# Down products whose operands begin elsewhere: split weights at 192, activations at 0 modulo 256 bytes

## The chip, the cores and the metric

The kernel runs on one core of one Trainium2 chip, from one program. The metric is the device time of one execution in microseconds (us). The kernel before takes 406.14 us, the median of three runs (405.77 to 406.33).

## The reference

One layer of a decoder for a sequence of S = 256 positions and a width of D = 1024, all in float32:

```
h = rmsnorm(x); proj = h @ w_in
x = x + (sigmoid(gA) * (o_A @ w_proj_nsa) + sigmoid(gB) * (o_B @ w_proj_dil)) @ w_out
h = rmsnorm(x)
u, gate = split(h @ w_up)            # w_up: 1024 x 5632
uc = conv_b + causal depthwise conv of width 3 over u
x = x + (gelu(uc) * gate) @ w_down   # w_down: 2816 x 1024
return rmsnorm(x)
```

o_A is a sparse attention (compressed, selected and sliding-window branches, gated), o_B a dilated attention over three groups. The change touches the last product but one line, `@ w_down`, alone.

## The kernel before

**Products in three parts.** Every float32 operand of a large product is split into a high part (`hi`, `ah`, `hTh`: the value rounded to the format fp32r) and a low part (the rest: `lo`, `al`, `hTl`). A product is then high x high + high x low + low x high, three matmuls that add up in PSUM. Names in the profile: `whi` and `wlo` are the split weights, `raw` the weights as they come from memory.

**Units.** The work is a list of units in the order of the program, each with one block of weights of 128 x 2048 numbers (1 MB). A unit's weights are loaded by a DMA of SP's queue into one of three `raw` buffers, split by ACT (`split_hi`, L128) and DVE (`split_lo`, L132) into one of three `whi` and three `wlo` buffers, and used by PE. Loads are issued five units ahead, the split runs one to two units ahead. `Unit` has a parameter `o`: the number of elements by which the unit's split weights begin behind the start of their buffers (buffers have 2240 elements, 2048 are used). Before, it is 32 in the three units of the values of the dilated attention (`vb`), and 0 elsewhere.

**Feed-forward part.** For each of NF = 11 blocks j of 256 hidden channels there are three units: two up products (for u and for gate) and one down product. The down product of block j - 2 stands behind the up products of block j, and the last two down products are computed at the end, by quarters of the output (function `last`).

- An up product is 2 x 8 x 3 = 48 matmuls (L177 and L182 in `parts`). The moving operand is hTh or hTl, 128 rows x 256 positions, and the stationary operand a piece of 128 x 128 of `whi` or `wlo`. They write `ps_d` for even j and `ps_o` for odd j.
- A down product is 48 matmuls too (L630 in `mm_down_part`). The moving operand is a row piece of 256 of `whi` or `wlo`, and the stationary one a piece of 128 x 128 of the activations `ah` or `al`. The same piece is loaded four times in succession, for four pieces of weights that go to four regions of PSUM, in `ps_s` or in the two `ps_t`.
- Between them the other engines work on the block: U = the scaled up product with two columns of zeros ahead (L581), C = the convolution (L585 on ACT, L589 on DVE) and its gelu (L596, L597), M = C times the gate (L604), and `ah`, `al` = its split (L614, L615).

A unit of `kick` in `parts` is one extra matmul of 64 columns ahead of a product, at two places of the program. It stays as it is.

**Where the tiles lie.** A matmul's operands are at a byte address in each partition of SBUF. By the built program, modulo 256:

| operands | before | after |
|---|---|---|
| up products: moving hTh, hTl | 192 | 192 |
| up products: stationary whi, wlo | 0 | 0 |
| down products: moving whi, wlo | 0 | 192 |
| down products: stationary ah, al | 64 | 0 |
| products of `vb` (o=32): moving whi, wlo; stationary hTh, hTl | 128; 192 | 128; 192 |
| third product (L177, ps_s): moving whi, wlo; stationary hTh, hTl | 0; 192 | 0; 192 |
| products for the merge and the output: moving oah, ob, mixh; stationary whi, wlo | 192; 0 | 192; 0 |
| C, M | 64 | 0 |
| U, its two buffers | 0, 32 | 0, 0 |

Each piece of an operand begins a multiple of 256 bytes behind the tile's start, so that a tile's number holds for all its pieces.

Of the kernel before, what the change touches and what calls it, by code (L numbers as in the profile page):

```python
# [11 lines left out]
F32 = mybir.dt.float32  # L12
# [6 lines left out]
S = 256  # L19
D = 1024  # L20
DFF = 2816
NF = DFF // 256
# [71 lines left out]
def build(ctx, tc, a, out):  # L94
# [9 lines left out]
    def pd(shape, tag="d"):  # L104
        return ps.tile([128] + shape, F32, name="ps_" + tag, tag=tag, bufs=1 if tag == "s" else 2)
# [91 lines left out]
    def CW(w, t):  # L197
        return sm_[:, 38 + 22 * w + t:39 + 22 * w + t]
# [29 lines left out]
    def bc(R, n):  # L228
        return R[:, None, :].to_broadcast([128, n, R.shape[-1]])
# [346 lines left out]
    def ev_u(j):  # L576
        def f(u):
            f_ = ffn["pool"]
            U = f_.tile([128, 2, S + 2], F32, name="U", tag="U", bufs=2)
            V.memset(U[:, :, 0:2], 0.0)  # L580
            V.tensor_tensor(out=U[:, :, 2:], in0=u.p, in1=bc(rt["R2"], 2), op=OP.mult)  # L581
            C = f_.tile([128, 2, S], F32, name="C", tag="C", bufs=2)
            for c in range(2):
                t = 2 * j + c
                A.activation(C[:, c], U[:, c, 2:], AF.Identity, scale=CW(2, t), bias=CB[:, t:t + 1])  # L585
            for w in (1, 0):
                for c in range(2):
                    t = 2 * j + c
                    V.scalar_tensor_tensor(C[:, c], U[:, c, w:w + S], CW(w, t), C[:, c], op0=OP.mult, op1=OP.add)  # L589
            ffn["C", j] = C  # L590
        return f
# [27 lines left out]
    def mm_down_part(u, j, tcs, c0=0, c1=512, own=None):  # L619

        wh, wl = w3(u, 2)
        h, l = ffn["a", j]
        half = [(0, 256), (256, 512)] if c1 - c0 == 512 else [(c0, c1)]
        start, seen = j == (0 if own is None else NF - 2), set()
        for n, (w, x) in enumerate(((wh, h), (wh, l), (wl, h))):
            for t in sorted({t for t, _ in tcs}):
                for kt in range(2):
                    for ch in [ch for q, ch in tcs if q == t]:
                        for b, e in half:
                            T.matmul(ffn["y"][t][ch][:, b:e] if own is None else own, x[:, kt, t * 128:t * 128 + 128],  # L630
                                     w[:, kt, ch * 512 + b:ch * 512 + e], start=start and (t, ch) not in seen,
                                     stop=j == NF - 1 and n == 2 and kt == 1, skip_group_check=True)
                            seen.add((t, ch))

    def mm_down(j):
        def f(u):
            if j == 0:
                s2 = pd([2, 512], "s")
                ta = pd([512], "t")
                tb = pd([512], "t")  # L640
                ffn["y"] = [[s2[:, 0], s2[:, 1]], [ta, tb]]
            if j < NF - 2:
                mm_down_part(u, j, [(t, ch) for t in range(2) for ch in range(2)])
        return f
# [12 lines left out]
        return f  # L657

    NFIRST = len(units)
    downs = [Unit(2048, mm_down(j)) for j in range(NF)]  # L660
    for j in range(NF + LAG):
        if j < NF:
            units.append(Unit(2048, mm_up(j, 0), ev_u(j)))
# [586 lines left out]
```

## Time and profile before

| | us |
|---|---|
| median of three runs | 406.14 |
| the profiled execution: its span from the first to the last instruction | 404.7 |
| PE busy / PE weight loads busy | 394.7 / 383.2 |
| DVE busy | 291.2 |
| ACT busy | 212.4 |
| POOL busy | 31.2 |
| first down product's first row in the chain of waits | at 248.32 |
| end of the last down matmul | at 397.7 |

The profiled execution's time beyond its span was not recorded, so the 1.4 us between its span and the median of the runs stand for what lies around the span.

How to read the rows: PE is the engine of the matmuls, PEld its loading of the stationary operand, which runs beside the matmuls. DVE, ACT and POOL are the vector, scalar and general engines, and SP issues DMAs. A row of the chain of waits has start, length, engine, tile, line and a count. Matmuls overlap in the pipeline, so the duration of one (277 ns, for instance) is not the time that it costs. What it costs is the time from one start to the next, and that is the length of a row of the chain divided by its count. A row of the grouped view has line, engine, operation, tiles, shapes and count, then busy us and mean ns of one, then the idle time ahead.

### The profile page before, as it was taken

The page shows a single profiled execution, that of the slowest core. Times are in us where ns is not written, and L with a number is a line of the kernel's source. Part 1 is how long each engine was busy: PE and PEld are TensorE (multiplying, and loading weights), DVE is VectorE, ACT ScalarE, POOL GpSimd, SP SyncE. Part 2 cuts the span into 40 slices and gives each one's busy share as a digit, 9 for nine tenths or more (in the row PEclk, how much of TensorE's full clock was granted, in tenths as well). Part 3 has the DMA queues.
Part 4 walks back from the last instruction along what each step waited for, and adds up shares of the span by engine and source line. Part 5 has one row for each costly group of instructions (what it writes and reads, how often), then busy time and mean ns, then how long its engine had stood idle before and what let it go on. Part 6 is the DMA issues. An engine that isn't in the chain of part 4 may idle for free.

```text
span 404.7 us, 8015 instructions
## 1 busy us (share of the span) xinstructions
PE 394.7 (98%) x3412; PEld 383.2 (95%) x3412; DVE 291.2 (72%) x486; ACT 212.4 (52%) x293; POOL 31.2 (8%) x58
## 2 busy tenths in 40 slices
PE   8999989999999999999999999999999999999993
PEld 6999989999998989999999999999999999999992
DVE  5879889887786557458897499676594774946853
ACT  5776764366664345663554765445264352643512
POOL 7100000000000000061143000000000000000012
PEclk9999999999999999999999999999999999999997
DMA  8965746345332532343556346662734726438002
GB/s 319 390 251 207 249 168 209 105 158 220 144 105 105 201 113 105 131 181 108 206 208 235 130 136 236 255 222 108 296 119 194 266 99 261 160 152 299 15 0 105
DMA packets 10980, 72.59 MB, mean 179 GB/s; under 512 B 1216, under 2 KB 1472, under 8 KB 2880
## 3 DMA queue, kind: packets, MB, share of 16 engines
q1 hardware_dynamic: 10512, 70.96, 48.2%
q10 hardware_dynamic: 432, 1.11, 0.7%
q8 instruction: 27, 0.44, 0.4%
q14 instruction: 9, 0.07, 0.1%
HBM read 71.02 MB, written 1.05 MB: 178 GB/s over the span
## 4 chain that ended last, share of the span: by engine, by line
PE 83%; DVE 10%; ACT 2%; DMA 2%; issue 1%; SPq 0%; POOLq 0%; POOL 0%; ACTq 0%
PE ps_d L177 25%; PE ps_d L182 12%; PE ps_o L177 9%; PE ps_s L630 8%; PE ps_t L630 7%; PE ps_o L182 5%; DVE wlo L132 4%; DMA first<-in_first_dram 2%; PE ps_t L177 2%; DVE hTl L202 2%; PE ps_d L344 2%; PE ps_o L905 2%; PE ps_s L946 1%; PE ps_t L892 1%; PE ps_d L280 1%
## 5 line engine op out<-in xcount | busy, mean ns | idle before, releaser
L132 DVE TENSOR_TENSOR wlo<-raw,whi 128x2048 fp32r<-128x2048 f32 (+2 forms) x61 | 135.2, 2217 | 4.2 <-ACT whi L128 4.2
L128 ACT ACTIVATE whi<-raw 128x2048 fp32r<-128x2048 f32 (+1 forms) x61 | 114.8, 1883 | 33.6 <-DMA raw<-in_wts_dram 28.8
L177 PE MATMUL ps_d<-hTh,whi 128*128 128x256 f32 x384 | 90.1, 280 | 0.0
L177 PE MATMUL ps_d<-hTl,whi 128*128 128x256 f32 x384 | 89.0, 277 | 0.0
L177 PEld LDWEIGHTS ps_d<-hTh,whi 128*128 128x128 f32 x384 | 72.2, 188 | 1.7 <-issue 1.3
L177 PEld LDWEIGHTS ps_d<-hTl,whi 128*128 128x128 f32 x384 | 72.2, 188 | 0.0
L182 PE MATMUL ps_d<-hTh,wlo 128*128 128x256 f32 x384 | 47.8, 277 | 0.0
L182 PEld LDWEIGHTS ps_d<-hTh,wlo 128*128 128x128 f32 x384 | 45.7, 188 | 0.0
L177 PE MATMUL ps_o<-hTh,whi 128*128 128x256 f32 x160 | 36.9, 277 | 0.0
L177 PE MATMUL ps_o<-hTl,whi 128*128 128x256 f32 x160 | 36.8, 276 | 0.0
L585 ACT ACTIVATE C<-U,small 128x256 f32<-128x256 f32 x22 | 12.0, 595 | 44.1 <-DVE U L581 44.1
L177 PEld LDWEIGHTS ps_o<-hTl,whi 128*128 128x128 f32 x160 | 30.1, 188 | 0.0
L177 PEld LDWEIGHTS ps_o<-hTh,whi 128*128 128x128 f32 x160 | 30.0, 188 | 0.0
L589 DVE SCALAR_TENSOR_TENSOR C<-U,small,C 128x256 f32<-128x256 f32 x44 | 19.4, 482 | 7.5 <-ACT C L585 7.4
L869 ACT ACTIVATE E<-E,ast 128x256 f32<-128x256 f32 (+1 forms) x32 | 14.2, 444 | 13.4 <-DVE ast L864 13.4
L581 DVE TENSOR_TENSOR U<-ps_d,R 128x512 f32<-128x512 f32 x6 | 4.1, 690 | 23.0 <-PE ps_d L182 19.2
L182 PE MATMUL ps_o<-hTh,wlo 128*128 128x256 f32 x160 | 19.8, 276 | 0.0
L132 POOL TENSOR_TENSOR wlo<-raw,whi 128x1024 fp32r<-128x1024 f32 x3 | 7.7, 2579 | 154.8 <-ACT whi L128 154.8
L182 PEld LDWEIGHTS ps_o<-hTh,wlo 128*128 128x128 f32 x160 | 18.9, 188 | 0.0
L581 DVE TENSOR_TENSOR U<-ps_o,R 128x512 f32<-128x512 f32 x5 | 3.4, 689 | 17.6 <-PE ps_o L182 17.6
L1207 POOL TENSOR_TENSOR tiny<-cst,tiny 128x1 f32<-128x1 f32 x2 | 1.4, 696 | 170.6 <-ACT sq L1206 170.6
L366 DVE TENSOR_TENSOR ML<-ps_d,R 128x512 f32<-128x512 f32 x8 | 5.5, 692 | 12.3 <-PE ps_d L182 12.3
(269 smaller groups left out, 762.5 us busy)
## 6 DMA issues: line engine op xcount, KB each, us to landing
raw<-in_wts_dram SPq DMA_DIRECT2D x61, 1024.0 KB, 4.8
first<-in_first_dram SPq DMA_DIRECT2D x2, 768.0 KB, 8.1
raw<-in_wts_dram SPq DMA_DIRECT2D x1, 1120.0 KB, 11.0
xn<-in_xn_dram SPq DMA_DIRECT2D x2, 512.0 KB, 12.4
xT<-in_xT_dram SPq DMA_DIRECT2D x1, 1024.0 KB, 6.9
first<-in_first_dram SPq DMA_DIRECT2D x2, 384.0 KB, 5.3
gf<-in_g_final_dram ACTq DMA_DIRECT2D x1, 512.0 KB, 3.7
out_dram<-X SPq DMA_DIRECT2D x1, 512.0 KB, 2.6
```

The costliest lines, as they stand in the source:

```text
L128: A.activation(u.hi[:, u.o + c0:u.o + c1], u.raw[:, c0:c1], AF.Copy)
L132: (eng or V).tensor_sub(u.lo[:, u.o + c0:u.o + c1], u.raw[:, c0:c1], u.hi.bitcast(F32)[:, u.o + c0:u.o + c1])
L177: T.matmul(po, l, r, start=start and bank not in banks, stop=False, skip_group_check=True)
L182: T.matmul(po, l, r, start=False, stop=stop and n == len(ks) - 1, skip_group_check=True)
L202: V.scalar_tensor_tensor(hTl[:, kt], x, g[:, kt:kt + 1], hTh.bitcast(F32)[:, kt], op0=OP.mult, op1=OP.subtract)
L344: T.matmul(u.p[:, i], l[:, kt, i * 128:i * 128 + 128], r[:, kt], start=kt == 0 and i == 0 and q == 0, stop=kt == 7 and q == 2, skip_group_ ...
L581: V.tensor_tensor(out=U[:, :, 2:], in0=u.p, in1=bc(rt["R2"], 2), op=OP.mult)
L585: A.activation(C[:, c], U[:, c, 2:], AF.Identity, scale=CW(2, t), bias=CB[:, t:t + 1])
L589: V.scalar_tensor_tensor(C[:, c], U[:, c, w:w + S], CW(w, t), C[:, c], op0=OP.mult, op1=OP.add)
L630: T.matmul(ffn["y"][t][ch][:, b:e] if own is None else own, x[:, kt, t * 128:t * 128 + 128], w[:, kt, ch * 512 + b:ch * 512 + e], start=st ...
L869: A.activation(self.E[:, i], self.E[:, i], AF.Exp, bias=mn[:, i:i + 1], scale=-1.0, accum_out=dn[:, i:i + 1])
L905: T.matmul(oA[js[c]][g * 64:g * 64 + 64, t * 128:(t + 1) * 128], Vn[:, k, b * 128 + g * 64:b * 128 + g * 64 + 64], self.PT[:, i], start=t ...
```

## The change

`downs`, the list of the eleven down units, gets `o=48`: their split weights begin 48 elements, 192 bytes, behind the start of the buffers. U's tile is allocated with 576 elements for each buffer instead of 2 x 258 = 516, and seen through a view of the same shape as before. It is followed in its pool by the tiles C, M, `ah` and `al`, which move by 448 bytes thereby, so that `ah` and `al` begin at 0 modulo 256. The instructions, their order and their waits are the same on all five engines; only addresses differ.

```diff
@@ ev_u @@
-            U = f_.tile([128, 2, S + 2], F32, name="U", tag="U", bufs=2)
+            U = f_.tile([128, 576], F32, name="U", tag="U", bufs=2)[:, :2 * S + 4].rearrange("p (c s) -> p c s", c=2)
             V.memset(U[:, :, 0:2], 0.0)
@@ build @@
-    downs = [Unit(2048, mm_down(j)) for j in range(NF)]
+    downs = [Unit(2048, mm_down(j), o=48) for j in range(NF)]
```

## The prediction

> **What bounds the kernel now.** I read the page's busy shares first, then the busy time by stretch of the feed-forward part, then the waits there, then the chain of waits in order of time. The page and the stretches (columns: stretch, length, busy time and count for PE, PEld, DVE, ACT, POOL, then granted clock, DMA share, GB/s):
>
> ```profile
> PE 394.7 (98%) x3412; PEld 383.2 (95%) x3412; DVE 291.2 (72%) x486; ACT 212.4 (52%) x293; POOL 31.2 (8%) x58
> ...
> 248.00:264.70 16.70, 16.70 (x147) 16.70 (x147) 12.72 (x13) 9.65 (x10) 0.00 (x0) 1.00 0.55 195
> 264.70:281.30 16.60, 16.60 (x147) 16.60 (x146) 11.01 (x14) 7.83 (x8) 0.00 (x0) 1.00 0.51 191
> ...
> 380.60:397.60 17.00, 17.00 (x146) 16.90 (x144) 11.17 (x14) 3.53 (x9) 2.35 (x4) 1.00 0.00 1
> ```
>
> From the first down product to the last, PE has no hole, at a granted clock of 1.00; per period DVE is busy 11.0 us of 16.6 and ACT 7.8. The waits of the same part, longest first, name POOL, ACT and DVE as waiters and nowhere PE:
>
> ```profile
> POOL tiny L1207 <- ACT sq L1206: 173.1, 4, 168.4
> ACT C L585 <- DVE U L581: 37.9, 8, 5.2
> ACT whi L128 <- DMA raw<-in_wts_dram: 24.4, 9, 4.1
> DVE U L581 <- PE ps_d L182: 19.2, 4, 4.8
> ```
>
> So here the time is the number of matmuls times the cadence at which PE starts them, and the only thing an address can change is the cadence. The chain of waits (start, length, engine, tile, line, count) gives it by dividing length by count:
>
> ```profile
> 242.88 3.63 PE ps_d L177 x32
> 246.50 1.82 PE ps_d L182 x16
> 248.32 0.94 PE ps_s L630 x8
> 249.26 0.94 PE ps_t L630 x8
> ...
> 253.97 3.65 PE ps_o L177 x32
> 257.62 1.81 PE ps_o L182 x16
> 259.43 3.63 PE ps_o L177 x32
> ...
> 270.53 3.65 PE ps_d L177 x32
> ...
> 369.85 3.65 PE ps_d L177 x32
> ...
> 386.40 2.83 PE ps_s L630 x24
> 389.23 2.83 PE ps_t L630 x24
> 392.05 2.84 PE ps_s L630 x24
> ```
>
> An up product runs at 3.63/32 = 113.4 ns per matmul. A down product has the same size of matmul (128 rows, 128 stationary columns, 256 moving ones) and runs at 0.94/8, or more finely 2.83/24 = 117.9 ns. That is 4.5 ns or 4% more, in all eleven down products. It shows as well in the durations of the groups, at equal shape:
>
> ```profile
> L177 PE MATMUL ps_o<-hTh,whi 128*128 128x256 f32 x160 | 36.9, 277 | 0.0
> L630 PE MATMUL ps_s<-whi,al 128*128 128x256 f32 x88 | 12.5, 281 | 0.0
> L630 PE MATMUL ps_t<-wlo,ah 128*128 128x256 f32 x84 | 12.0, 281 | 0.0
> ```
>
> **Is the slow cadence a matter of addresses?** Up products stream hTh and hTl, which begin at 192 modulo 256 bytes, against stationary weights at 0. Down products stream weights at 0 against stationary activations at 64. But pairs of one and the same kind are found at both cadences in the mixer stage:
>
> ```profile
> 30.03 3.63 PE ps_t L177 x32
> ...
> 166.37 0.81 PE ps_t L975 x6
> 167.17 3.77 PE ps_d L177 x32
> 170.94 1.88 PE ps_d L182 x16
> ...
> 176.68 1.81 PE ps_d L177 x16
> ...
> 218.86 2.10 PE ps_d L280 x16
> 221.30 2.93 PE ps_d L280 x24
> ```
>
> The L177, L182 and L280 rows all stream from 192 against stationary at 0. At 30.03 and 176.68 the cadence is 113 ns; at 167.17 it is 3.77/32 = 117.8 and at 170.94 1.88/16 = 117.5, as slow as the down products. So (192, 0) has two cadences, each of which holds for many matmuls. The slow one begins behind a stop of PE: the stretch at 221.30 follows a hole, and before the one at 167.17 stand short transposes of the attention, at 166.37. [...] Going into a down product, the cadence falls from 113.4 to 117.9 within it with no wait. Coming out, the first 32 matmuls take 3.65 instead of 3.63 us, 0.02 more, and then 113.4 is back. A switch of tiles at equal residues does no harm: 237.44 to 248 passes over two weight tiles at 113.4 throughout.
>
> ```profile
> 237.44 3.63 PE ps_d L177 x32
> 241.06 1.81 PE ps_d L182 x16
> ```
>
> **The change part by part.** No instruction moves. What changes is where the operands begin: down weights at 192, activations at 0, which are the residues of the up products on either side. From the up product at 226 to the last down product at 397 no residue jumps any more, and PE never stops. If the fast phase stands at 248, as it does in the row at 246.50, nothing that I can name turns it into the slow one.
>
> Down products: 11 of 48 matmuls, 528 in all (88 and 84 per group in the rows above, three groups each, and the last 12 in another tile). Price of each: from 117.9 to 113.4, 4.5 ns. 528 x 4.5 ns = 2.38 us. Bounds per matmul: no gain if the cadence is the down product's own; 4.5 ns if it becomes that of an up product. In the other direction, the third product streams weights at 0 against hTh at 192:
>
> ```profile
> 17.95 2.06 PE ps_s L177 x16
> ```
>
> That is 128.8 ns for 280 columns; at the fast rate per column it would be 113.4 x 280/256 = 124.0. An unfavourable pair thus costs 4.8 ns, about what the down product already pays, so I give the downs' own cadence no further loss. I take the full 4.5 ns, because the new pair is exactly that of the neighbouring rows.
>
> The way out of a down product: eight down products are followed by an up product (the first at 253.97, the last at 369.85), and each loses 0.02 us at 3.65 against 3.63. Without a jump that goes too: 8 x 0.02 = 0.16 us.
>
> [...]
>
> Writing the split weights 192 bytes further: the values' products (o=32, so 128 bytes off) already write so. The hi split (ACT, first row those around the values' products, second row the feed-forward part) and the lo split (DVE, in the same order) take the same there (min/median/max ns):
>
> ```profile
> L128 ACT ACTIVATE whi<-raw x4: 1899/1904/1906, 69.9 to 94.3; 128x2048 fp32r<-128x2048 f32 x4
> L128 ACT ACTIVATE whi<-raw x24: 1898/1905/1925, 254.8 to 379.4; 128x2048 fp32r<-128x2048 f32 x24
> L132 DVE TENSOR_TENSOR wlo<-raw,whi x5: 2285/2286/2287, 68.9 to 102.3; 128x2048 fp32r<-128x2048 f32 x5
> L132 DVE TENSOR_TENSOR wlo<-raw,whi x23: 2279/2283/2287, 254.0 to 378.4; 128x2048 fp32r<-128x2048 f32 x23
> ```
>
> U's two buffers begin at residues 0 and 32 now and take turns with ps_d and ps_o, so their rows compare the two:
>
> ```profile
> L581 DVE TENSOR_TENSOR U<-ps_d,R x6: 682/691/692, 225.1 to 375.3; 128x512 f32<-128x512 f32 x6
> L581 DVE TENSOR_TENSOR U<-ps_o,R x5: 681/691/692, 235.1 to 358.8; 128x512 f32<-128x512 f32 x5
> ```
>
> No difference. C and M move from 64 to 0, which no row shows; by these rows I take nothing. The cover for all of it is DVE's 5.6 free us per period.
>
> Does a faster PE run into a wait? A period becomes 0.23 us shorter. The tightest supply is the lo half of an up product, which DVE finishes at 253.97 + 2.28 = 256.25 and which PE first loads at 257.35:
>
> ```profile
> 253.97 2.28 DVE L132 TENSOR_TENSOR wlo<-raw,whi 128x2048 fp32r<-128x2048 f32 x1
> ...
> 257.35 1.89 PEld L182 LDWEIGHTS ps_o<-hTh,wlo 128*128 128x128 f32 x16
> ```
>
> 1.1 us of slack, renewed in each period, since DVE and ACT are paced by PE and have time left. If that cover went, each period would lose what is missing. The weights come at 191 GB/s with the DMA engines at 0.51; 1.4% faster is 194. What follows the last matmul (397.7 to 404.7) stays.
>
> Sum: 2.38 + 0.16 = 2.54 us. Span: 404.7 - 2.5 = 402.2. The median of the runs, 406.14, lies 1.4 above the profiled span, so 402.2 + 1.4 = **403.6 us**.
>
> **The rivals.** (A) *The cadence is the down product's own*: four matmuls in turn load the same stationary tile and write four different PSUM regions, which no fast row does, and the addresses have no part in it. For it: all down rows are slow, even at 386 where there are no up products between. Against it: exactly the same 117.8 in plain products, at 167.17, with no such form, and slow phases hold on once entered, so the rows at 386 prove nothing. At its price of zero: 406.1 us. [...]
>
> (B) *Slower: the phase is lost and never won back.* Something within the first down product (its changing PSUM regions, say) throws PE into the slow phase at 248. Today the jump behind each down product brings the up products back to 113.4. With equal residues there is no jump, and the slow phase stays, as it did over the 48 matmuls from 167.17 on. The price: eight pairs of up products of 96 matmuls, 768 x 4.5 ns = 3.46 us lost, the 0.16 won, the down products as they were: 406.1 + 3.3 = 409.4 us. It decides from the first slow up product on: where the slow phase came only in the middle, at 320, the first half would be won (1.3 us) and half of the loss would stand against it (1.7). Against it: within 237 to 248 no switch starts it.
>
> (C) *A part of it*: fast cadence, but a few matmuls at each border of 4 to 8 ns or a short hole somewhere, or the slow phase in the last two down products alone, 96 x 4.5 = 0.43 us. This gives 403.8 to 405.2.
>
> **How the numbers follow.** Forecast 0.72, with its own range 403.0 to 404.3; (C) 0.07; (A) 0.12, at 405.8 to 406.4; (B) 0.09, at 407 to 410. About 0.2%, or 0.8 us, is what a measurement of this kernel tells from no change. Faster than that are the forecast and nearly all of (C): 0.78. Within it are (A) and a trace of (C): 0.13. Slower is (B): 0.09. The range 402.9 to 405.7 holds the forecast and (C), and leaves (A) and (B) out. Its lower end is the forecast less the spread of the runs (405.77 to 406.33).
>
> **What would show it.** In the chain of waits six rows of a down product would read 0.90 or 0.91 instead of 0.94, x24 would take 2.72 instead of 2.83, and 3.65 behind a down product would become 3.63; the mean of L630's matmuls would go from 281 to 276 or 277. From the first down product to the last up product every period would be 16.3 us. (A) shows unchanged L630 rows with 3.65 or 3.63 beside them. (B) shows 3.77 in rows of L177 after 254. The forecast is wrong if PE appears among the waiters of the feed-forward part, or if L630 stays at 117.9 ns.

## The result, and the profile after

The changed kernel takes 403.88 us, the median of five runs (403.25 to 404.07), against 406.15 for the kernel before on the same chip (405.77 to 406.38). The ratio is 0.9938, with a 95% interval from 0.9927 to 0.9949. Forecast were 403.6 us, and a range of 402.9 to 405.7. The span of the profiled execution falls from 404.7 to 402.3 us, by 2.4 us. Of all the kernels here, only the last of the experiments had slow executions, three of its eight, at 409.6 to 412.3 us, and its median and ratio leave them out.

The chain of waits of the changed kernel (start, length, engine, tile, line, count), at the places shown of before:

```profile
246.47 1.81 PE ps_d L182 x16
248.28 0.91 PE ps_s L630 x8
249.19 0.91 PE ps_t L630 x8
...
253.72 3.63 PE ps_o L177 x32
257.35 1.81 PE ps_o L182 x16
259.16 3.63 PE ps_o L177 x32
...
384.28 2.72 PE ps_s L630 x24
387.00 2.72 PE ps_t L630 x24
389.72 2.73 PE ps_s L630 x24
```

A row of eight down matmuls takes 0.91 us instead of 0.94, and 24 of them 2.72 instead of 2.83: 113.3 ns per matmul, the cadence of the up products. The row behind a down product, at 253.72, is 3.63 instead of 3.65. The groups by shape say the same of the durations, 276 ns instead of 281 (the row of the up products stays at 277):

```profile
L630 PE MATMUL ps_s<-whi,al 128*128 128x256 f32 x88 | 12.1, 276 | 0.0
...
L630 PE MATMUL ps_t<-wlo,ah 128*128 128x256 f32 x84 | 11.6, 276 | 0.0
```

The stretches show that nothing else became a bound, and that the granted clock is 1.00 as it was before, so the clock isn't what changed: PE is busy through all of a period of 16.3 us, and DVE has 5.3 us left in the second one (columns: stretch, length, PE, PEld, DVE, ACT, POOL, granted clock, DMA share, GB/s).

```profile
248.00:264.30 16.30, 16.30 (x146) 16.30 (x145) 12.56 (x13) 9.50 (x10) 0.00 (x0) 1.00 0.53 197
264.30:280.60 16.30, 16.30 (x146) 16.30 (x145) 10.95 (x13) 7.76 (x8) 0.00 (x0) 1.00 0.54 194
```

### The profile page after: what moved, and what is told of

Read it like the earlier page. It is cut to its first block, busy times and chain, and to the rows that moved or that the text cites. A ratio compares the mean times of both kernels' runs of the same rounds, so it can differ in the third digit from the quotient of the medians.

```text
span 402.3 us, 8015 instructions
## 1 busy us (share of the span) xinstructions
PE 392.3 (98%) x3412; PEld 381.0 (95%) x3412; DVE 291.3 (72%) x486; ACT 212.4 (53%) x293; POOL 31.1 (8%) x58
## 4 chain that ended last, share of the span: by engine, by line
PE 83%; DVE 10%; ACT 2%; DMA 2%; issue 1%; SPq 0%; POOLq 0%; POOL 0%; ACTq 0%
PE ps_d L177 25%; PE ps_d L182 12%; PE ps_o L177 9%; PE ps_s L630 7%; PE ps_t L630 7%; PE ps_o L182 5%; DVE wlo L132 4%; DMA first<-in_first_dram 2%; PE ps_t L177 2%; DVE hTl L202 2%; PE ps_d L344 2%; PE ps_o L905 2%; PE ps_s L946 1%; PE ps_t L892 1%; PE ps_d L280 1%
## 5 line engine op out<-in xcount | busy, mean ns | idle before, releaser
L177 PE MATMUL ps_d<-hTh,whi 128*128 128x256 f32 x384 | 90.0, 280 | 0.0
L177 PE MATMUL ps_d<-hTl,whi 128*128 128x256 f32 x384 | 89.0, 277 | 0.0
L177 PEld LDWEIGHTS ps_d<-hTh,whi 128*128 128x128 f32 x384 | 72.2, 188 | 1.7 <-issue 1.3
L177 PEld LDWEIGHTS ps_d<-hTl,whi 128*128 128x128 f32 x384 | 72.2, 188 | 0.0
L182 PE MATMUL ps_d<-hTh,wlo 128*128 128x256 f32 x384 | 47.8, 277 | 0.0
L182 PEld LDWEIGHTS ps_d<-hTh,wlo 128*128 128x128 f32 x384 | 45.7, 188 | 0.0
L177 PE MATMUL ps_o<-hTh,whi 128*128 128x256 f32 x160 | 36.9, 277 | 0.0
L177 PE MATMUL ps_o<-hTl,whi 128*128 128x256 f32 x160 | 36.8, 276 | 0.0
L177 PEld LDWEIGHTS ps_o<-hTl,whi 128*128 128x128 f32 x160 | 30.0, 188 | 0.0
L177 PEld LDWEIGHTS ps_o<-hTh,whi 128*128 128x128 f32 x160 | 30.0, 188 | 0.0
L182 PE MATMUL ps_o<-hTh,wlo 128*128 128x256 f32 x160 | 19.8, 276 | 0.0
L182 PEld LDWEIGHTS ps_o<-hTh,wlo 128*128 128x128 f32 x160 | 18.9, 188 | 0.0
```

Source lines behind the costliest of these rows:

```text
L177: T.matmul(po, l, r, start=start and bank not in banks, stop=False, skip_group_check=True)
L182: T.matmul(po, l, r, start=False, stop=stop and n == len(ks) - 1, skip_group_check=True)
```

## The experiments

The theory under test, J: a pair of operands has more than one cadence; which of them holds, called the phase here (113.3 ns the fast one, 117.8 the slow one at the pair (192, 0)), is kept from matmul to matmul, and a stop of PE or a jump of the residues can change it. Rivals are named with each run. The residues of a pair, the places modulo 256 bytes where its two operands begin, are written as (moving, stationary), and its difference is moving minus stationary. A jump is a change of residues from one product to the next, and a border is the change between an up and a down product.

### One half of the change at a time

Weights alone, so that the down products are at (192, 64):

```diff
-    downs = [Unit(2048, mm_down(j)) for j in range(NF)]
+    downs = [Unit(2048, mm_down(j), o=48) for j in range(NF)]
```

> The half of the change on the weights: down products at (moving 192, stationary 64). Theory J (two phases, and a jump of either residue at the border throws PE out of the fast one): the stationary operand still jumps from 0 to 64, so the down products stay at about 117.9 ns, the time at 406.1. Rival M (the moving operand's start alone decides, 192 is good and 0 is bad): 113.4 ns and 403.9 us. Rival D (the down product's own form): is dead if any kernel but the whole change is fast, and after the whole change it has already fallen.

Activations alone, so that they are at (0, 0):

```diff
-            U = f_.tile([128, 2, S + 2], F32, name="U", tag="U", bufs=2)
+            U = f_.tile([128, 576], F32, name="U", tag="U", bufs=2)[:, :2 * S + 4].rearrange("p (c s) -> p c s", c=2)
```

> The half of the change on the activations: down products at (moving 0, stationary 0). Theory J: the moving operand still jumps from 192 to 0; 117.9 ns, 406.1 us. Rival M (the moving operand's start alone decides): 117.9 ns too. Rival S (the stationary operand's start alone decides, 0 is good): 113.4 ns and 403.9 us. Rival C (equal residues of both operands collide in each matmul): above 118 ns, and 407 us or more.

Measured: the weights alone give 406.64 us, ratio 1.0015 (0.9997 to 1.0033) to the kernel before; the activations alone 407.07, ratio 1.0018 (1.0005 to 1.0030). The chain of waits of the first kernel:

```profile
386.72 2.85 PE ps_s L630 x24
```

And of the second:

```profile
253.58 0.96 PE ps_t L630 x8
254.54 3.65 PE ps_o L177 x32
...
387.66 2.88 PE ps_s L630 x24
```

That is 118.8 ns at (192, 64) and 120.0 ns at (0, 0). Neither the moving operand's start alone (rival M) nor the stationary one's (rival S) makes a down product fast, and neither half brings anything (with the activations alone the kernel is even 0.9 us slower). But (0, 0) isn't at the 117.9 ns of before either, as J without further rules would have it, so rival C (equal residues) is right about the time of its own case, 120.0 ns and 407.07 us; that the operands collide no run shows. The pair of equal residues has a cadence that (0, 64) didn't show.

### The slow pair without the jump

Down products stay at (0, 64) as in the kernel before; hTh and hTl begin at 0 and the weights of the up products and of the mixer's products with hTh at 64 (at 192 for the values), so that up and down products are alike:

```diff
-    hTh = const.tile([128, 8, S], F32R, name="hTh")
-    hTl = const.tile([128, 8, S], F32R, name="hTl")
+    hTh = const.tile([128, 8 * S + 16], F32R, name="hTh")[:, 16:].rearrange("p (k s) -> p k s", k=8)
+    hTl = const.tile([128, 8 * S + 48], F32R, name="hTl")[:, :8 * S].rearrange("p (k s) -> p k s", k=8)
...
-            units.append(Unit(2048, mm_up(j, 0), ev_u(j)))
+            units.append(Unit(2048, mm_up(j, 0), ev_u(j), o=16))
```

> Down products at (0, 64) as before, but the up products beside them at (0, 64) too (hTh and hTl begin at 0, their weights at 64), so that no residue jumps inside the feed-forward part; the same for the products of the mixer with hTh and hTl, which changes its phases too, so only the cadences of the feed-forward part are compared. Theory J: one cadence for up and down products from the second block on, since nothing throws PE out of a phase; if the phase at 226 us is the fast one, 113.4 ns for L630, with the pair that was slow before. Rival P (the pair of residues decides, and (0, 64) is a slow pair): L630 at 117.9 and L177, L182 there at 117.9 as well.

Measured: 403.87 us in one run, a span of 402.0. The chain of waits:

```profile
247.99 0.91 PE ps_s L630 x8
248.90 0.91 PE ps_t L630 x8
...
253.43 3.63 PE ps_o L177 x32
...
383.99 2.72 PE ps_s L630 x24
```

The down products have the addresses' residues of the kernel before and the cadence of the kernel after. So (0, 64) is no slow pair, and rival P falls: what made it slow before was the way into it. In this one execution the whole gain in the feed-forward part is had without touching the operands of the down products, by moving those of their neighbours.

### A third pair with the same difference, and the jump

Down products at (64, 128) between up products at (192, 0):

```diff
-            U = f_.tile([128, 576], F32, name="U", tag="U", bufs=2)[:, :2 * S + 4].rearrange("p (c s) -> p c s", c=2)
+            U = f_.tile([128, 528], F32, name="U", tag="U", bufs=2)[:, :2 * S + 4].rearrange("p (c s) -> p c s", c=2)
-    downs = [Unit(2048, mm_down(j), o=48) for j in range(NF)]
+    downs = [Unit(2048, mm_down(j), o=16) for j in range(NF)]
```

> Down products at (moving 64, stationary 128): a third pair in which the moving operand begins 64 below the stationary one modulo 256, as in (192, 0) and (0, 64). Up products stay at (192, 0), so both residues jump at every border, by 128 each. Theory J, with what the first four kernels add to it (a pair of difference -64 has a fast and a slow phase; a jump can throw PE into the slow one): L630 at 117.8 ns from the first matmuls on and 0.02 us lost behind each down product, 406.1 us. Rival Q (only pairs that touch 0 as the moving start suffer, or only jumps of 64): 113.4 ns and 403.9 us.

Measured: 406.17 us in one run, beside 406.19 for the kernel before. Its chain of waits is that of the kernel before, row by row to 0.01 us, 2.83/24 = 117.9 ns and 3.65 behind the down product:

```profile
252.64 0.95 PE ps_t L630 x8
253.59 3.65 PE ps_o L177 x32
...
386.07 2.83 PE ps_s L630 x24
```

The jump, not the start at 0, goes with the slow phase; rival Q falls.

### Other differences without a jump

All products of the feed-forward part at (0, 0), from the kernel with hTh at 0: the units' `o` is 0 again, and U has the size that brings the activations to 0.

```diff
-            units.append(Unit(2048, mm_up(j, 0), ev_u(j), o=16))
+            units.append(Unit(2048, mm_up(j, 0), ev_u(j)))
```

> Both operands at 0 in up and down products (hTh, hTl, the split weights and the activations all begin at 0), so that nothing jumps in the feed-forward part but the difference of the residues is 0 instead of -64; the mixer's products with hTh are at (0, 0) as well. Theory J in its strict form (only jumps and stops matter): 113.4 ns for L177, L182 and L630. Theory R (the difference of the residues sets which cadences a pair has, and a jump only chooses among them): 120.0 ns for all of them, as the down products alone had it when they were at (0, 0); 22 up and 11 down products of 48 matmuls by 6.6 ns more, 10 us, and as many in the mixer by some 4 us: 415 us or more.

All of them with the moving operand 96, and then 32, below the stationary one instead of 64, from the changed kernel (the weights beside hTh at 32 or 224, and the activations too; for 96):

```diff
-            units.append(Unit(2048, mm_up(j, 0), ev_u(j)))
+            units.append(Unit(2048, mm_up(j, 0), ev_u(j), o=8))
...
-            h = f_.tile([128, 2, S], F32R, name="ah", tag="ah", bufs=4)
+            h = f_.tile([128, 2 * S + 64], F32R, name="ah", tag="ah", bufs=4)[:, 8:8 + 2 * S].rearrange("p (c s) -> p c s", c=2)
```

> From the changed kernel: the stationary operands beside hTh, and those of the down products, begin at 32 instead of 0, the moving ones stay at 192 (those of the values' products at 96 beside hTh's 192), so the moving operand begins 96 below the stationary one modulo 256 instead of 64, everywhere in the feed-forward part and in most of the mixer. Theory R (the difference sets the cadences that a pair can have): one cadence for L177, L182 and L630 in the feed-forward part, between 109 and 120 ns, which -64 doesn't have: at 116 ns 3.8 us more there. A difference of no consequence within 32 bytes would leave 113.4 ns and 403.9 us.

> The same with the stationary operands at 224, so that the moving one begins 32 below the stationary one modulo 256 (values' products 160 beside 192). Theory R: a cadence of its own between those of -64 (113.4 or 117.8 ns) and of 0 (120.0 ns); at 117 ns some 5 us more in the feed-forward part than 403.9. If both this and -96 are slower than 113.4, -64 is the best of the seen ones; if one of them is faster or has no slow phase in the mixer, it beats the changed kernel.

Measured, one run each: 418.95 us at a difference of 0, 414.08 at -96 and 413.64 at -32, beside 406.2 to 406.5 for the kernel before. The chain of waits at difference 0:

```profile
255.65 0.96 PE ps_t L630 x8
...
260.45 3.84 PE ps_o L177 x32
```

At -96, first in the mixer and then in the feed-forward part:

```profile
24.07 3.76 PE ps_t L177 x32
...
257.21 3.80 PE ps_o L177 x32
```

And at -32:

```profile
257.09 3.79 PE ps_o L177 x32
```

Per matmul of 256 columns the rows of the feed-forward part give 120.0, 118.8 and 118.4 ns, in up and down products alike and from block to block. The row at 24.07 belongs to the mixer, where the same pair (192, 32) holds 3.76/32 = 117.5 ns: the difference of -96 has two cadences too, where one was expected. No run shows the 109 ns at the lower end of the range expected there; the rows gave 118.8 and 117.5. Theory J in its strict form (only jumps and stops matter) falls with the first of the three kernels. What they show agrees with theory R, by which the difference of the residues sets the cadences that a pair can have. That it is the difference, and not the single pair, is shown for -64 alone, by three pairs, since each of the others was tried in the feed-forward part with one pair. Of the differences tried, only -64 showed the 113.3 ns. The mixer pays too, so the whole times are far above the feed-forward part's share.

### Is a phase inherited?

The extra matmul of 64 columns at 226 us, which the kernel has behind a stop of PE, taken out of the changed kernel:

```diff
-        if i in (24, NFIRST + 2):
+        if i == 24:
             rt["kick"] = "own"
```

> The changed kernel without the extra matmul of 64 columns ahead of the second block's up product (at 226 us), which follows a stop of PE. Theory J: if PE comes out of that stop in the slow phase, nothing wins the fast one back, as no residue jumps: all 1488 matmuls from 226 us on at 117.9 ns, some 6.5 us longer than with it, 410 us. If it comes out in the fast one, 403.9. Rival P (the pair (192, 0) is a fast pair whenever PE doesn't stop): 113.4 ns and 403.9 us at any rate.

Measured: 403.74 us, ratio 0.9926 (0.9897 to 0.9955). PE came out of the stop in the fast phase without help:

```profile
227.24 3.64 PE ps_o L177 x32
230.88 1.81 PE ps_o L182 x16
```

So this run tells nothing on the question, except that this extra matmul earns nothing here that can be measured. In all eleven traces in which the pairs around 226 us have the difference -64, with the extra matmul or without it, PE comes out of this stop in the fast phase: the first 16 matmuls of L182 behind it take 1.81 us in each, 113.1 ns per matmul. Other stops are less certain. The kernel with the weights alone has the same instructions and addresses in the mixer as the changed kernel, and yet two products there, each behind a short stop, have exchanged their phases. The rows are the last 16 matmuls of each, in the changed kernel first and then in the one with the weights alone:

```profile
63.44 1.81 PE ps_d L182 x16
...
71.83 1.89 PE ps_d L182 x16
```

```profile
63.61 1.88 PE ps_d L182 x16
...
71.95 1.82 PE ps_d L182 x16
```

Which phase such a product takes can thus differ from one execution to the next.

The disturbance was then put where PE is surely in the fast phase, ahead of the up product for u of the sixth block:

```diff
-        if i in (24, NFIRST + 2):
+        if i in (24, NFIRST + 2, NFIRST + 13):
             rt["kick"] = "own"
```

> The changed kernel with one extra matmul of 64 columns ahead of the sixth block's up product for u (near 286 us), where PE is in the fast phase. Its own cost is about a quarter to a full matmul, 0.03 to 0.1 us. Theory J with inheritance: if that disturbance throws PE into the slow phase, everything behind it up to 397 us stays slow, 960 matmuls by 4.5 ns, 4.3 us more, and none of it comes back at a border. If PE stays in the fast phase or returns to it in a few matmuls, 404.0 us, and then a single disturbance is harmless and the rival of a lost phase had no ground here.

Measured: 408.15 us in one run, 4.3 us above the changed kernel. The chain of waits, around the extra matmul (L172) and at the end:

```profile
284.25 0.91 PE ps_s L630 x8
285.16 0.91 PE ps_t L630 x8
286.06 0.03 PE ps_o L172
286.10 3.85 PE ps_o L177 x32
289.94 1.88 PE ps_o L182 x16
291.83 3.77 PE ps_o L177 x32
...
387.94 2.83 PE ps_s L630 x24
390.76 2.83 PE ps_t L630 x24
```

The matmul itself takes 0.03 us on the chain, and the row behind it has 3.85 instead of 3.77, 0.08 us more. Whether the matmul or this delay lost the phase can't be told apart. From there on, every product of the feed-forward part is at 3.77/32 = 117.8 or 2.83/24 = 117.9 ns, up and down, at the very addresses that ran at 113.3 before it, for 100 us and over 960 matmuls. None of it comes back between up and down products, where no residue jumps now. In the kernel before, the fast phase came back at each border behind a down product (3.65, then 3.63). What the forecast's rival of a lost phase describes thus happened in this one execution. It did not in the changed kernel, where the second matmul behind the extra one of 226 us starts 204 ns behind the first and 113 to 114 ns are back within five matmuls: such a delay need not lead to the slow phase.

### Winning the fast phase in the mixer

Six products of the mixer with 48 matmuls each run at 117.8 ns in the traces of both kernels. An extra matmul of 64 columns ahead of each:

```diff
-        if i in (24, NFIRST + 2):
+        if i in (11, 13, 17, 20, 21, 23, 24, NFIRST + 2):
             rt["kick"] = "own"
```

> The changed kernel with an extra matmul of 64 columns ahead of the six products of the mixer that run in the slow phase (at 68, 84, 118, 143, 152 and 167 us). Theory J: like the one at 226 us, each can win the fast phase: 6 x 48 x 4.5 ns = 1.3 us gained, less 6 x 0.05 to 0.1 us for the matmuls themselves: 402.9 to 403.1 us, ratio near 0.992. Rival (what follows the attention's short matmuls is decided elsewhere, and an extra matmul changes nothing): 404.2 us.

Measured: 403.97 us, ratio 0.9944 (0.9927 to 0.9961) to the kernel before. No gain over the changed kernel, against what was expected from J. In the trace, three of the six (the products that began at 68, 84 and 167 us) run at 113 to 114 ns and three (at 118, 143 and 152) stay slow: their last 16 matmuls take 1.81 to 1.82 us in the first three and 1.88 to 1.89 in the others. Only the three that ran fast:

```diff
-        if i in (24, NFIRST + 2):
+        if i in (11, 13, 23, 24, NFIRST + 2):
```

> The changed kernel with the extra matmul of 64 columns ahead of those three products of the mixer alone that it brought into the fast phase (at 68, 84 and 167 us). Theory J: 3 x 0.21 us gained, less 3 x 0.08 us for the extra matmuls, 0.4 us: 403.5 us, ratio near 0.993 to the kernel before. Rival: the extra matmuls and their holes cost what they win: 403.9 us.

Measured: 403.71 us, ratio 0.9934 (0.9916 to 0.9953). The interval of the changed kernel, 0.9927 to 0.9949, covers it: a gain of 0.4 us can't be told from none. In this trace the product at 59 us is slow and the one at 68 us fast, which is what the kernel with the weights alone shows without an extra matmul; so in this trace only the products at 84 and 167 us can owe their phase to the extra matmuls.

With these three, the third product's weights were begun at 128 instead of 0, which makes its difference -64 (before it is 0 - 192 = 64):

```diff
-UW = 2240
+UW = 2304
...
-    units.append(Unit(2240, mm_third, ev_v))
+    units.append(Unit(2240, mm_third, ev_v, o=32))
```

> The changed kernel with the three useful extra matmuls of the mixer, and with the third product's weights begun at 128 instead of 0 beside hTh at 192 (the split buffers are 64 elements larger for it), so that its difference is -64 instead of 64. Theory R: its 48 matmuls of 280 columns fall from 128.9 ns to 124 (fast phase) or stay near 128 (slow phase, since it follows the first units, which run at 117.8): 0.2 us gained or nothing; 403.5 us, ratio near 0.993 to the kernel before. If the part of the three extra matmuls and this one both count, the time is below the changed kernel's 403.9 by 0.4 to 0.6 us; if they cost what they win, it is the same.

Measured: 404.78 us, the median of five executions (403.53 to 405.5), ratio 0.9961 (0.9944 to 0.9979): by its median slower than the changed kernel, with intervals that just overlap, so that a loss isn't shown by the times. The chain of waits of the profiled execution, 404.78 us:

```profile
17.57 2.07 PE ps_s L177 x16
19.64 1.02 PE ps_s L182 x8
...
24.19 3.77 PE ps_t L177 x32
27.96 1.89 PE ps_t L182 x16
29.85 3.77 PE ps_t L177 x32
...
43.12 3.77 PE ps_d L177 x32
...
196.22 3.77 PE ps_o L177 x32
```

And of the changed kernel at the same place:

```profile
17.91 2.06 PE ps_s L177 x16
...
24.54 3.63 PE ps_t L177 x32
28.17 1.81 PE ps_t L182 x16
29.98 3.63 PE ps_t L177 x32
...
42.85 3.64 PE ps_d L177 x32
```

The third product's own rows don't move: 2.07/16 = 129 ns. The last matmuls ahead of it (L344, ahead of the rows shown) run in the slow phase in both traces, at 117.8 ns from start to start in the changed kernel and 0.59/5 = 118 ns here. In the changed kernel the third product at (0, 192) is followed by the fast phase. Here, at (128, 192), the slow one goes on behind it, up to 48.8 us, with rows of 3.77 instead of 3.63 us. So an equal difference isn't the same as equal residues: between (128, 192) and (192, 0) both still jump by 64, and in this execution the jump won nothing. Other traces have faster first units, that of the kernel with the three extra matmuls alone among them (92 matmuls of L344 in 10.79 us against 11.18 here), so this loss may not come in every execution.

The row at 196.22 is a second loss, at the pair (192, 0), with no jump and no extra matmul just ahead. The product before it (L546) takes 5.48 us for 48 matmuls, where 113.3 ns each would make 5.44, and all 144 matmuls of L177 and L182 behind it up to 213 us are at 117.5 to 117.8 ns. In the changed kernel one matmul of L546 starts 123 ns behind the one ahead of it instead of 113, and 113.3 is back within four matmuls. A delay of at most 0.04 us can thus go with the loss of a phase, and one of 0.01 need not.

No version beat the changed kernel by more than can be measured.

## Why the prediction was right

**The bound.** Right: PE has no hole in the feed-forward part before or after, and its cadence alone changed.

**528 matmuls by 4.5 ns, 2.38 us.** Right in kind and size: 117.9 to 113.3 ns in each row of L630.

**0.16 us at eight borders.** Right in kind: 3.65 became 3.63 behind each down product. From the start of the first down product's row to the end of the last row of 24 matmuls, the chain takes 146.57 us before (248.32 to 394.89) and 144.17 after (248.28 to 392.45): 2.40 us. That stretch holds 504 of the 528 down matmuls, for which the two terms give 504 x 4.5 ns + 0.16 us = 2.43 us, so both are borne out.

**Other engines.** Right: the splits take what they took (ACT 1902 to 1923 ns, DVE 2279 to 2287), and no wait of PE appeared.

**403.6 against 403.88.** The span was right: forecast were 402.2 us, and the execution of the median had 402.1. What lay around the span was 1.8 us in each of the five executions (the profiled one took 404.07 with a span of 402.3), and not 1.4, because the forecast had set the span of one execution against the median of others.

**The jump and the phase.** That a jump of the residues makes the down products slow was my reading of the rows of before, and it held where the runs tried it. The pair of before is fast without the jump (113.3 ns), another pair is slow with it (117.9), and a phase is kept for 100 us. Three things the reading lacked. The difference of the residues goes with the cadences that were seen (0: 120.0; -32: 118.4; -96: 118.8, or 117.5 in the mixer; -64: 113.3 or 117.8). A single extra matmul, with 0.08 us more in the row behind it, was enough to lose the phase in one execution. And which phase follows a stop isn't fixed (1.81 or 1.88 us for the same 16 matmuls). That the new pair equals the neighbours' was the ground of the forecast, and that is what decided it. That the fast phase stands at 248 us was a premise, taken from one row; all eleven traces at the difference -64 bear it out (1.81 or 1.82 us for the 16 matmuls ahead of the first down product), so it wasn't luck as far as they go.

**The third product.** The prediction read its 128.8 ns as the price of an unfavourable pair, against 124.0 for 280 columns at the fast rate. It had 129 ns at the difference -64 too, so that reading isn't borne out; no term of the sum hung on it.

**The rivals.** (A), the down product's own form, fell: its four matmuls on one stationary tile run at 113.3. The residues do make a difference here, of 4.5 to 6.7 ns above the 113.3. (B), the lost phase, didn't occur in the changed kernel, but the run with the extra matmul at 286 us shows its price: 4.3 us for 960 matmuls, 4.5 ns each. Whether a chance of 0.09 was fair, one outcome can't tell: in the changed kernel no wait of PE stands between 248 and 397 us.

The runs show that the cadence depends on both operands' residues (113.3 to 120.0 ns) and on what ran before (113.3 or 117.8 ns at (192, 0)), and not where the nanoseconds are lost. No run tests the modulus of 256 bytes itself. Why jumps from (192, 0) to (0, 64) and (64, 128) lead to the slow phase and those back, or from (0, 192) to (192, 0), to the fast one, and why that from (128, 192) to (192, 0) left it slow, stays open. The kernels that show the jump and its absence were traced in one execution each; within each trace all down products agree.

## What to carry to other kernels

Where PE never waits, divide the length of a row of the chain by its count for each kind of matmul: equal shapes at different cadences mean time that no engine's busy share shows (here PE was busy through the whole stretch at 117.9 ns as at 113.3). Look then at the start of both operands modulo 256 bytes, keep their difference at the value of the fastest rows (-64 here, 113.3 ns against 118.4 to 120.0 at the others in the feed-forward part), and give neighbouring products the same pair if the phase ahead is fast; where it is slow, a jump can be worth keeping. Verify it in the rows of the neighbours as well, since in one run here a lost phase cost 4.5 ns in each of the 960 matmuls behind it.

## What was not expected of the hardware

A single matmul of 64 columns, 0.03 us on the chain with 0.08 more in the row behind it, in the middle of an undisturbed stream cost 4.3 us, because the 960 matmuls behind it went from 113.3 to 117.8 ns and stayed there. In another trace a product of 48 matmuls that took 0.04 us more than at 113.3 ns was followed by the same loss in 144 matmuls of L177 and L182. And two kernels with the operands' difference at -32 and -96 instead of -64 took 413.6 and 414.1 us where the changed kernel takes 403.9, though operands had moved by 32 bytes only.
